# The steps of the late modulation sums, bound to their place in POOL's order

## The chip, the cores and the metric

The kernel runs on one core of a Trainium2 chip. The core has a matrix engine (PE, whose weight loads are shown apart as PEld), a vector engine (DVE), a scalar engine (ACT), a general engine (POOL) and a sync engine (SP) that here does nothing but issue transfers. Each engine takes its instructions strictly in the order in which they stand in its program; engines wait for each other, and for transfers, by semaphores. The metric is the time of one execution on the device in microseconds (us). Before the change the median of three runs is 1459.89 us (1458.16 to 1461.62).

## The reference

One layer of a diffusion backbone: two token mixers (differential attention and a multi-scale pooling) joined by gates, then an MLP with a squared ReLU. 256 latent tokens and 256 context tokens, width 2048, MLP width 8192, all in float32. Six vectors, computed from the conditioning vector `c`, shift, scale and gate the stream:

```python
mod = (jax.nn.silu(c) @ w_mod[l] + b_mod[l])[:, None, :]
sa, ca, ga, sm, cm, gm = jnp.split(mod, 6, axis=-1)
...
h = modulate(x, norm_attn_w[l], sa, ca)          # rmsnorm * (1 + ca) + sa
p = h @ w_in[l]
...
x = x + ga * mix
x = x + gm * sq_relu_mlp(modulate(x, norm_mlp_w[l], sm, cm), w_ff1[l], w_ff2[l])
```

`sa` and `ca` are needed at the very start. The other four, `ga`, `cm`, `sm` and `gm`, are needed late: `ga` when the mixed tokens have been projected, `cm` and `sm` for the second norm, `gm` in the last lines of the MLP. Each is a product of one row of 2048 with a 2048 x 2048 matrix; this document is about how these four are summed.

## The kernel before

**Products.** Every float32 weight tile is split in two parts: `whi` (rounded, by ACT, L245) and `wlo` (the rest, by DVE, L246). Three matmuls stand for one float32 product (high by high, low by high, high by low). PE reads the weights in chunks of 128 x 1024; `wchunk` loads, splits and hands out the next chunk, with two chunks of lookahead, six `raw` buffers for arriving weights and three buffers each for `whi` and `wlo`. All chunks stand in one list, `stream`, in the order of their use.

**Stages.** In order of time: the first products, which make the modulated input (to some 130 us); the products for v, q and k with the attention heads between them (to some 330 us); pooling; the gates, whose products are named `pg` and `pyy` (some 385 to 660 us); the output projection `wo` (to some 740 us); then the MLP, which goes through eight blocks. In a block, `ff1(b)` makes 1024 hidden columns in four parts: PE multiplies (L1035, L1038), ACT takes the ReLU (L1045), POOL squares it (`rsq`, L1046), ACT and DVE split the square (L272, L273) into the operand `act` for `ff2(b)`, which comes after (L454, L455, L460).

**The late sums.** `late_gen` works on `ga`, `cm`, `sm` and `gm` between the chunks of the main stream, half a vector (1024 columns) at a time. For each of 16 weight tiles, DVE adds `weights * silu(c)` to a 128 x 1024 tile (`late_part`, L628 and L630). That leaves 128 partial rows, which have to be added up across partitions. `late_fold` does that by transfers that add to their destination: rows 64 to 127 are added to rows 0 to 63, then 32 to 16, and so on down to one row (seven steps, L635); this row is added to a row in DRAM that holds the bias (L638), and the row is read back into all 128 partitions (L641). For `cm`, `late_norm` stands between these, with two transfers and two small POOL operations (L646 to L649). The tiles are `ga_bc` (both halves of `ga`), `sb` (`cm` and `sm`) and `gm_bc`. Each of the eight halves so needs nine transfers or more, every one of which has to land before the next can be issued. All are issued by POOL: a transfer that has to wait for the one before it makes all of POOL wait, and whatever stands behind it in POOL's program.

**What sets the order.** Steps of the fold are put off with `later(n, fn)`: `fn` runs after `n` more weight chunks have been handed out, and writes its instructions into the program at that place. A list scheduler then orders each engine's program by its own estimate of when each instruction is ready. An instruction wrapped in `pin` (`keep_in_program_order`) keeps its place with respect to the rest of the program instead. Before the change the `late_fold` transfers are not pinned. Most other work on POOL that the document speaks of is not pinned either: the rotary additions `qraw` (L485) and the squares `rsq`.

Of the kernel before, what the change touches and what calls it, by code (L numbers as in the profile page):

```python
# [14 lines left out]
ALU = mybir.AluOpType  # L15
AX = mybir.AxisListType

P = 128
# [30 lines left out]
def layer(ctx: ExitStack, tc, a, out):  # L49
    nc = tc.nc  # L50
# [4 lines left out]
    pin = tc.keep_in_program_order  # L55
# [41 lines left out]
    def later(n, fn):  # L97

        waiting.append([n, fn])
# [426 lines left out]
    cols = {}  # L526
# [70 lines left out]
    def late_gen():  # L597
        for name in ("ga", "cm", "sm", "gm"):
            if name == "ga":
                dst = ga_bc  # L600
            elif name == "gm":
                mods["gm"] = None
                yield
                mods["gm"] = s8("gm_bc", [P, D])
                dst = mods["gm"]
            else:
                if "sb" not in mods:
                    mods["sb"] = s16("sb", [P, 2, D])
                dst = mods["sb"][:, 0 if name == "cm" else 1, :]
            for half in range(2):  # L610
                yield
                o = dst[:, half * 1024:half * 1024 + 1024]
                norm_w = pr("nmw")[:, 8 * half:8 * half + 8] if name == "cm" else None
                for k in range(KT):
                    raw = raw_chunk(a["w_" + name][half, k])
                    later(2 if credit_rate[0] < 1 else 1, partial(late_part, o, raw, k))
                    if k == 8:
                        row = rows.tile([1, 1024], F32, tag="row", name="row")
                        nc.gpsimd.dma_start(row, a["b_" + name][half])
                    if k == KT - 1:  # L620
                        wait = 40 - 26 * half if name == "ga" else 2 if credit_rate[0] < 1 else 1
                        later(wait, partial(late_fold, o, row, norm_w, P // 2, 2 if name == "sm" else 3))
                    yield
# [8 lines left out]
    def late_fold(o, row, norm_w, n, step):  # L632

        if n > 0:
            nc.gpsimd.dma_start(o[0:n, :], o[n:2 * n, :], accum_op=ALU.add)  # L635
            later(step, partial(late_fold, o, row, norm_w, n // 2, step))
            return
        nc.gpsimd.dma_start(row, o[0:1, :], accum_op=ALU.add)  # L638
        if norm_w is not None:
            later(1, partial(late_norm, row, norm_w))  # L640
        later(2 if norm_w is None else 3, lambda: nc.gpsimd.dma_start(o, row.broadcast_to([P, 1024])))  # L641

    def late_norm(row, norm_w):

        cols = pool.tile([P, 8], F32, tag="nmc", name="nmc")
        nc.gpsimd.dma_start(cols, row.rearrange("o (p c) -> (o p) c", c=8))  # L646
        gp.tensor_scalar(cols, cols, 1.0, None, ALU.add)
        gp.tensor_mul(cols, cols, norm_w)
        nc.gpsimd.dma_start(row.rearrange("o (p c) -> (o p) c", c=8), cols)  # L649
# [536 lines left out]
```

## Time and profile before

| | |
|---|---|
| median of three runs | 1459.89 us |
| the profiled execution | 1465.34 us, with a span of 1463.6 us |
| granted clock of PE, mean over the span | 0.996 |
| busy share of DVE, ACT, POOL | 67%, 46%, 12% |
| bytes moved by transfers | 355.23 MB, 243 GB/s in the mean |

The page of a profile sums one execution; the views behind it list instructions by time, by line or by tile. In a list of instructions in order of time, the columns are the start (us from the span's start), the duration, the engine, the line and operation, output and input; in square brackets stands how long the engine sat idle before it, and what ended the wait. In a list of waits the columns are the total in us, the number of waits and the longest. Where a stretch of time is tabulated, each engine's busy time is followed by its count of instructions, and the last three columns are PE's granted clock (1.00 is full speed), the busy share of the 16 DMA engines and GB/s. POOL's transfers are shown with the time it takes to issue them, not to carry them out.

### The profile page before, as it was taken

How to read it: one execution, taken by the hardware profiler on the slowest of the kernel's cores; microseconds unless marked ns; L12 is line 12 of the kernel's file. 1: busy time of each engine (PE TensorE's matmuls, PEld its weight loads, DVE VectorE, ACT ScalarE, POOL GpSimd, SP SyncE). 2: the span in 40 equal slices, each digit the busy share in tenths (PEclk: the TensorE clock that was granted, in tenths of full speed). 3: DMA queues.
4: the chain of work that ended last, by engine and by line, in shares of the span. 5: the costliest groups of instructions: out<-in, count | busy, mean ns of one | idle time of the engine just before them, and what ended most of it. 6: DMA issues, size and time to landing. Idle time of an engine off the chain costs nothing.

```text
span 1463.6 us, 19756 instructions
## 1 busy us (share of the span) xinstructions
PE 1435.7 (98%) x7448; PEld 1181.9 (81%) x7448; DVE 983.3 (67%) x1218; ACT 670.4 (46%) x901; POOL 173.1 (12%) x192
## 2 busy tenths in 40 slices
PE   6999989999999999999999999999999999999998
PEld 4667877778888888888878888888888788888887
DVE  4567785668788778787767656656666465555675
ACT  4235335556654444444545545445354353544432
POOL 1001111102310121110101100110000100000260
PEclk9999999999999999999999999999999999999999
DMA  9996693335589999999646677777777665565563
GB/s 374 408 408 248 212 324 112 101 116 163 174 297 332 339 329 340 333 348 332 226 153 225 231 235 236 245 237 247 243 233 240 199 198 193 188 194 193 185 195 124
DMA packets 100976, 355.23 MB, mean 243 GB/s; under 512 B 12864, under 2 KB 13520, under 8 KB 100880
## 3 DMA queue, kind: packets, MB, share of 16 engines
q1 hardware_dynamic: 96624, 345.19, 68.5%
q0 software_dynamic: 4256, 8.77, 2.6%
q8 instruction: 58, 0.95, 0.3%
q14 instruction: 38, 0.31, 0.1%
HBM read 347.61 MB, written 2.17 MB: 239 GB/s over the span
## 4 chain that ended last, share of the span: by engine, by line
PE 84%; DMA 10%; issue 2%; DVE 1%; ACT 1%; POOL 1%; SPq 0%; DVEq 0%; POOLq 0%; ACTq 0%
PE f L1035 13%; PE f L455 8%; PE f L454 8%; PE f L460 8%; PE f L1038 7%; DMA raw<-in_w_m_dram 6%; PE pg L455 4%; PE pg L454 4%; PE pg L460 4%; DMA gm_bc<-gm_bc 2%; PE pyy L455 2%; PE v L455 2%; PE pyy L460 2%; PE pyy L454 2%; PE v L454 2%
## 5 line engine op out<-in xcount | busy, mean ns | idle before, releaser
L246 DVE TENSOR_TENSOR wlo<-raw,whi 128x1024 fp32r<-128x1024 f32 (+1 forms) x430 | 533.2, 1243 | 339.5 <-ACT whi L245 309.4
L245 ACT CAST whi<-raw 128x1024 fp32r<-128x1024 f32 (+1 forms) x430 | 449.9, 1047 | 558.4 <-PE f L455 184.7
L1035 PE MATMUL f<-h,whi 128*128 128x512 f32 x896 | 225.9, 395 | 3.1 <-ACT whi L245 3.1
L455 PE MATMUL f<-whi,act 128*128 128x512 f32 x512 | 199.5, 390 | 0.0
L454 PE MATMUL f<-whi,act 128*128 128x512 f32 x512 | 199.3, 389 | 0.0
L1035 PEld LDWEIGHTS f<-h,whi 128*128 128x128 f32 x896 | 162.6, 190 | 32.6 <-ACT whi L245 3.3
L460 PE MATMUL f<-wlo,act 128*128 128x512 f32 x512 | 136.9, 389 | 0.0
L1038 PEld LDWEIGHTS f<-h,wlo 128*128 128x128 f32 x896 | 122.6, 191 | 8.8
L1038 PE MATMUL f<-h,wlo 128*128 128x256 f32 x896 | 125.1, 283 | 0.0
L460 PEld LDWEIGHTS f<-wlo,act 128*128 128x128 f32 x512 | 96.1, 188 | 19.9
L455 PEld LDWEIGHTS f<-whi,act 128*128 128x128 f32 x512 | 96.2, 188 | 19.8
L454 PEld LDWEIGHTS f<-whi,act 128*128 128x128 f32 x512 | 96.1, 188 | 19.7
L454 PE MATMUL pg<-whi,hL 128*128 128x512 f32 x256 | 100.8, 394 | 0.0
L455 PE MATMUL pg<-whi,hL 128*128 128x512 f32 x256 | 99.8, 390 | 0.0
L1046 POOL TENSOR_TENSOR rsq<-relu 128x512 f32<-128x512 f32 x28 | 29.2, 1042 | 432.3 <-ACT relu L1045 422.1
L630 DVE SCALAR_TENSOR_TENSOR sb<-raw,sil,sb 128x1024 f32<-128x1024 f32 x60 | 76.8, 1280 | 0.0
L460 PE MATMUL pg<-wlo,hL 128*128 128x512 f32 x256 | 68.5, 389 | 0.0
L455 PEld LDWEIGHTS pg<-whi,hL 128*128 128x128 f32 x256 | 48.1, 188 | 10.1 <-issue 0.2
L454 PEld LDWEIGHTS pg<-whi,hL 128*128 128x128 f32 x256 | 48.1, 188 | 10.1 <-issue 0.2
L460 PEld LDWEIGHTS pg<-wlo,hL 128*128 128x128 f32 x256 | 48.1, 188 | 10.0
L1060 DVE TENSOR_TENSOR acc<-f,acc 128x512 f32<-128x512 f32 x48 | 30.9, 686 | 20.5 <-PE f L460 20.5
L635 POOL DMA_DIRECT2D sb<-sb x28 | 22.2, 791 | 186.7 <-DMA sb<-sb 121.2
(283 smaller groups left out, 2182.8 us busy)
## 6 DMA issues: line engine op xcount, KB each, us to landing
raw<-in_w_ff_dram SPq DMA_DIRECT2D x240, 512.0 KB, 4.2
raw<-in_w_m_dram SPq DMA_DIRECT2D x64, 512.0 KB, 10.2
raw<-in_w_ga_dram SPq DMA_DIRECT2D x32, 512.0 KB, 4.4
raw<-in_w_gb_in_dram SPq DMA_DIRECT2D x32, 512.0 KB, 5.1
raw<-in_w_cm_dram SPq DMA_DIRECT2D x32, 512.0 KB, 5.5
raw<-in_w_ga_in_dram SPq DMA_DIRECT2D x32, 512.0 KB, 5.5
raw<-in_w_sm_dram SPq DMA_DIRECT2D x32, 512.0 KB, 5.5
raw<-in_w_o_dram SPq DMA_DIRECT2D x32, 512.0 KB, 5.5
```

Source lines behind the costliest of these rows:

```text
L245: act.copy(hi, raw)
L246: vec.tensor_sub(lo, raw, hi.bitcast(F32))
L454: pe.matmul(banks[t], tok(h, k, 0, tt), wt, start=k == 0, stop=False)
L455: pe.matmul(banks[t], tok(h, k, 1, tt), wt, start=False, stop=False)
L460: pe.matmul(banks[t], tok(h, k, 0, tt), wt, start=False, stop=k == 2 * nk - 1)
L630: pin(vec.scalar_tensor_tensor(o, raw, sil[:, 0, k:k + 1], o, ALU.mult, ALU.add))
L635: nc.gpsimd.dma_start(o[0:n, :], o[n:2 * n, :], accum_op=ALU.add)
L1035: pe.matmul(ps, hi[:, kk * P:kk * P + P], both(h2, k), start=k == 0, stop=False)
L1038: pe.matmul(ps[:, T:2 * T], lo[:, kk * P:kk * P + P], act_slice(h2, k, 0), start=False, stop=k == KT - 1)
L1046: gp.tensor_mul(sq, r, r)
L1060: vec.tensor_add(acc[:, t, gs], bs[t], acc[:, t, gs])
```

## The change

All transfers of `late_fold` and the first of `late_norm` are wrapped in `pin`, so that they keep the place at which the program writes them. What is computed, the number of instructions and the operations are the same.

```diff
     def late_fold(o, row, norm_w, n, step):
         if n > 0:
-            nc.gpsimd.dma_start(o[0:n, :], o[n:2 * n, :], accum_op=ALU.add)
+            pin(nc.gpsimd.dma_start(o[0:n, :], o[n:2 * n, :], accum_op=ALU.add))
             later(step, partial(late_fold, o, row, norm_w, n // 2, step))
             return
-        nc.gpsimd.dma_start(row, o[0:1, :], accum_op=ALU.add)
+        pin(nc.gpsimd.dma_start(row, o[0:1, :], accum_op=ALU.add))
         if norm_w is not None:
             later(1, partial(late_norm, row, norm_w))
-        later(2 if norm_w is None else 3, lambda: nc.gpsimd.dma_start(o, row.broadcast_to([P, 1024])))
+        later(2 if norm_w is None else 3, lambda: pin(nc.gpsimd.dma_start(o, row.broadcast_to([P, 1024]))))

     def late_norm(row, norm_w):
         cols = pool.tile([P, 8], F32, tag="nmc", name="nmc")
-        nc.gpsimd.dma_start(cols, row.rearrange("o (p c) -> (o p) c", c=8))
+        pin(nc.gpsimd.dma_start(cols, row.rearrange("o (p c) -> (o p) c", c=8)))
```

The programs of PE, DVE, ACT and SP keep their order; only POOL's differs, in four places. The first two belong together. Before, the nine transfers of `ga`'s first half stand between the rotary additions of the second group of query heads; in POOL's program of before, that place reads (a number behind a name tells tiles of one name apart):

```order
L485 TENSOR_TENSOR qraw_1321<-qraw_1321,qsq_1323 128x512
L635 DMA ga_bc_1341<-ga_bc_1341 64x1024
L635 DMA ga_bc_1341<-ga_bc_1341 32x1024
L635 DMA ga_bc_1341<-ga_bc_1341 16x1024
L635 DMA ga_bc_1341<-ga_bc_1341 8x1024
L485 TENSOR_TENSOR qraw_1836<-qraw_1836,qsq_1838 128x512
L635 DMA ga_bc_1341<-ga_bc_1341 4x1024
L485 TENSOR_TENSOR qraw_1856<-qraw_1856,qsq_1858 128x512
L635 DMA ga_bc_1341<-ga_bc_1341 2x1024
```

In the changed program the additions follow each other, and the transfers of both halves of `ga` stand in the gates, alternating, behind the last POOL operation of the attention (`osq`); this is the head of that place in POOL's new program, where the first row of 64x1024 belongs to the first half and the second one to the second half:

```order
L728 TENSOR_SCALAR osq_3670<-osq_3670 128x512
L635 DMA ga_bc_1341<-ga_bc_1341 64x1024
L635 DMA ga_bc_1341<-ga_bc_1341 32x1024
L635 DMA ga_bc_1341<-ga_bc_1341 16x1024
L635 DMA ga_bc_1341<-ga_bc_1341 8x1024
L635 DMA ga_bc_1341<-ga_bc_1341 64x1024
L635 DMA ga_bc_1341<-ga_bc_1341 4x1024
L635 DMA ga_bc_1341<-ga_bc_1341 32x1024
L635 DMA ga_bc_1341<-ga_bc_1341 2x1024
L635 DMA ga_bc_1341<-ga_bc_1341 16x1024
```

So nine transfers have moved from the attention to the gates, from before two rotary additions to a place where POOL computes nothing. The end of the second half (its last addition, its row, its broadcast) has moved behind the first transfers of `sb`.

The third and fourth places are the two folds of `gm_bc` in the MLP. Before, the second one stands in one piece ahead of four squares of an MLP block; in POOL's program of before:

```order
L635 DMA gm_bc_6622<-gm_bc_6622 4x1024
L635 DMA gm_bc_6622<-gm_bc_6622 2x1024
L635 DMA gm_bc_6622<-gm_bc_6622 1x16x64
L638 DMA row_9067<-gm_bc_6622 16x1x64
L641 DMA gm_bc_6622<-row_9067 128x1024
L1046 TENSOR_TENSOR rsq2_9978<-relu_9979 128x512
L1046 TENSOR_TENSOR rsq2_10082<-relu_10083 128x512
L1046 TENSOR_TENSOR rsq2_10187<-relu_10188 128x512
```

In the changed program the same transfers stand between the squares:

```order
L635 DMA gm_bc_6622<-gm_bc_6622 8x1024
L1046 TENSOR_TENSOR rsq2_9978<-relu_9979 128x512
L635 DMA gm_bc_6622<-gm_bc_6622 4x1024
L1046 TENSOR_TENSOR rsq2_10082<-relu_10083 128x512
L635 DMA gm_bc_6622<-gm_bc_6622 2x1024
L635 DMA gm_bc_6622<-gm_bc_6622 1x16x64
L1046 TENSOR_TENSOR rsq2_10187<-relu_10188 128x512
L638 DMA row_9067<-gm_bc_6622 16x1x64
L1046 TENSOR_TENSOR rsq2_10291<-relu_10292 128x512
L641 DMA gm_bc_6622<-row_9067 128x1024
```

Five of the nine steps have moved behind one or more of the block's squares. The first fold of `gm_bc` moves in the same way, by four steps.

## The prediction

> **What bounds the kernel now.** I read the page first, then PE's list of waits, then the lists in order of time around each wait. The page says that PE is the engine that counts; its waits say where time can still be won.
>
> ```profile
> span 1463.6 us, 19756 instructions
> PE 1435.7 (98%) x7448; PEld 1181.9 (81%) x7448; DVE 983.3 (67%) x1218; ACT 670.4 (46%) x901; POOL 173.1 (12%) x192
> ...
> PE qkT L492 <- POOL qraw L485: 4.0, 1, 4.0
> PE f L1035 <- ACT whi L245: 3.1, 1, 3.1
> ```
>
> PE is idle for 1463.6 - 1435.7 = 27.9 us. Most of that lies at the start and the end, where the change does nothing. Behind the first 130 us the list has two waits of weight, 4.0 and 3.1 us, each of them a single event. The first one names POOL. The second names ACT, and has to be followed back to whom ACT waited for.
>
> **The first wait.** Here are DVE's rotary product that feeds the fifth addition, the rows of POOL around that addition, and PE's.
>
> ```profile
> 207.28 0.69 DVE L484 TENSOR_TENSOR qraw<-qraw,tabs 128x512 f32<-128x512 f32 x1
> ...
> 198.19 0.90 POOL L635 DMA_DIRECT2D ga_bc<-ga_bc  x1 [39.77 <-DMA raw<-in_w_ga_dram]
> ...
> 216.69 0.81 POOL L635 DMA_DIRECT2D ga_bc<-ga_bc  x1 [3.75 <-DMA ga_bc<-ga_bc]
> 217.24 1.55 POOL L485 TENSOR_TENSOR qraw<-qraw,qsq 128x512 f32<-128x512 f32 x1
> ...
> 213.72 1.13 PE L693 MATMUL sc<-kT,qT 64*128 64x512 f32 x4
> 218.85 0.79 PE L492 MATMUL qkT<-prm,qraw 128*128 128x128 f32 x4 [4.00 <-POOL qraw L485]
> 219.29 0.77 PE L454 MATMUL k<-whi,hL 128*128 128x512 f32 x1
> 219.86 0.63 PE L455 MATMUL k<-whi,hL 128*128 128x512 f32 x1
> 220.29 0.63 PE L454 MATMUL k<-whi,hL 128*128 128x512 f32 x1
> ...
> 222.77 0.39 PE L454 MATMUL k<-whi,hL 128*128 128x512 f32 x1
> 223.00 0.39 PE L455 MATMUL k<-whi,hL 128*128 128x512 f32 x1
> ```
>
> The addition's data were there at 207.28 + 0.69 = 207.97 us. It ran at 217.24, since four transfers of the fold stood ahead of it, from 198.19 to 216.69, each waiting until the last had landed. PE wanted its transposes at 213.72 + 1.13 = 214.85 and got them at 218.85. Then it ran slow for a while: matmuls started 0.43 us apart (219.86, 220.29), and 0.23 us apart later (222.77, 223.00). From 218.85 to 222.77 it did four transposes and eight matmuls in 3.92 us; at full speed the eight take 8 x 0.23 = 1.84, and with the 0.55 us or so that I estimate for the transposes the same work is 2.4. So the wait cost 4.0 + 1.5 = 5.5 us. With the transfers gone the addition can run from 208.0 to 209.5, over 5 us before PE asks. What is late next? The transposes stand behind `sc`, which is PE's own work, so nothing is left to wait for there: **-5.5 us**.
>
> **The second wait.** ACT waits in the MLP, for POOL:
>
> ```profile
> 1071.31 1.04 POOL L1046 TENSOR_TENSOR rsq<-relu 128x512 f32<-128x512 f32 x1 [53.65 <-ACT relu L1045]
> 1082.48 1.04 POOL L1046 TENSOR_TENSOR rsq<-relu 128x512 f32<-128x512 f32 x1 [10.13 <-ACT relu L1045]
> ...
> 1129.74 0.85 POOL L635 DMA_DIRECT2D gm_bc<-gm_bc  x1 [23.87 <-DVE gm_bc L630]
> ...
> 1167.95 0.58 POOL L641 DMA_DIRECT2D gm_bc<-row  x1 [1.59 <-DMA row<-gm_bc]
> 1168.54 1.06 POOL L1046 TENSOR_TENSOR rsq<-relu 128x512 f32<-128x512 f32 x1
> ...
> 1252.66 1.04 POOL L1046 TENSOR_TENSOR rsq<-relu 128x512 f32<-128x512 f32 x1 [53.65 <-ACT relu L1045]
> ...
> 1340.87 1.04 POOL L1046 TENSOR_TENSOR rsq<-relu 128x512 f32<-128x512 f32 x1 [53.65 <-ACT relu L1045]
> ...
> 1169.63 0.62 ACT L272 CAST act<-rsq 128x512 fp32r<-128x512 f32 x1 [9.31 <-POOL rsq L1046]
> ...
> 1171.25 3.54 PE L1035 MATMUL f<-h,whi 128*128 128x512 f32 x8 [3.09 <-ACT whi L245]
> ...
> 1175.71 2.00 PE L1035 MATMUL f<-h,whi 128*128 128x512 f32 x8
> ```
>
> The first square of an MLP block comes every 88.21 us when nothing is in the way (1340.87 - 1252.66). After the one at 1071.31 the next was due at 1159.5. It came at 1168.54, 9.0 us late, because the whole fold, from 1129.74 to 1167.95, stood ahead. ACT's split of that square was 9.31 us late, ACT's cast of the next weights stood behind the split, and PE waited 3.09 us and then took 3.54 us for eight matmuls that take 2.00. What it cost in all is read from the blocks: 1252.66 - 1071.31 = 181.35, against 2 x 88.21 = 176.42: 4.9 us. With the new order the first square stands behind the step of eight rows. The fold starts at 1129.74, and four steps of some 5 us each (the median of a landing is 5.1, quoted below) end by 1150, before 1159.5. Each later square has at most two steps ahead of it, and the squares come 11.17 us apart (1082.48 - 1071.31): **-4.9 us**. What hides the waits that the change adds here (a square behind a step) is this gap: it is gone if one step takes over 5 us longer than it does now. The fold ends some 30 us later than now, near 1200.
>
> The first fold of `gm_bc` has the same shape, yet PE's list shows no wait for it:
>
> ```profile
> 985.03 1.06 POOL L1046 TENSOR_TENSOR rsq<-relu 128x512 f32<-128x512 f32 x1
> ...
> 986.12 0.62 ACT L272 CAST act<-rsq 128x512 fp32r<-128x512 f32 x1 [2.23 <-POOL rsq L1046]
> ```
>
> There ACT was held up by 2.23 us only, and PE's weights were split ahead by more than that. Nothing is to be had: 0.
>
> **What the moved transfers cost where they go.** Nine transfers land in the gates, beside those of the second half.
>
> ```profile
> q0 software_dynamic: 4256, 8.77, 2.6%
> ...
> 416.00:420.00 4.00, 4.00 (x19) 3.34 (x18) 4.00 (x5) 1.80 (x2) 0.17 (x1) 1.00 0.80 260
> 420.00:424.00 4.00, 4.00 (x19) 3.30 (x19) 3.67 (x4) 1.05 (x1) 0.60 (x1) 1.00 0.83 272
> 424.00:428.00 4.00, 4.00 (x20) 3.30 (x19) 3.07 (x5) 1.97 (x2) 0.78 (x1) 1.00 0.90 352
> ...
> 425.70 1.05 ACT L245 CAST whi<-raw 128x1024 fp32r<-128x1024 f32 x1 [3.50 <-PE pg L460]
> ...
> 428.22 0.39 PE L454 MATMUL pg<-whi,hL 128*128 128x512 f32 x1
> ...
> 540.85 1.05 ACT L245 CAST whi<-raw 128x1024 fp32r<-128x1024 f32 x1 [1.66 <-PE pg L455]
> ...
> 547.00 0.39 PE L454 MATMUL pyy<-whi,yb 128*128 128x512 f32 x1
> ...
> L898 DVE TENSOR_TENSOR xtmp<-wo,ga_bc x6: 683/688/693, 676.4 to 723.0; 128x512 f32<-128x512 f32 x6
> ```
>
> POOL's queue (q0) takes 2.6% of the span of all 16 DMA engines, 38 us, for eight halves: at most 4.8 us a half. I counted ACT's casts against PE's chunks through the gates: the cast that ends at 426.75 is for the chunk that PE starts at 428.22. That margin of 1.47 us is the smallest of the stage; the cast that ends at 541.90 is for the chunk of 547.00, 5.1 us ahead, and most are so from there on. In the changed order the large steps of the second half (64 and 32 rows) fall there, at about 416 to 428, since the halves now take turns. They are the larger part of the 4.8 us; from 416 to 428 the DMA engines have 0.8 + 0.7 + 0.4 = 1.9 us to spare. My estimate is 2.5 us of extra transfer work, against 1.9 + 1.47 = 3.4 to hide it: nothing is left over, and I take 0. The other bound: all 4.8 us arrive late, PE waits 4.8 - 1.5 = 3.3 us, and 1.7 us of slow clock follow, **+5.0 us**. A gain there I exclude, since PE does not idle in the gates now. `ga` is late next, but has time: its first reader (L898) starts at 676, and the second half's broadcast, now behind two steps of `sb`, should be out by 490. `sb` itself loses a microsecond or two to the transfers put between its own, and each of its halves starts with DVE's next sum, not with the fold before.
>
> **The sum** is -5.5 - 4.9 = -10.4 us: 1465.34 - 10.4 = 1454.9 in a profiled execution. The profiled one is 5.45 us above the median of the runs shown. I take the change off that median: 1459.89 - 10.4 = **1449.5 us**.
>
> **A rule weighed.** The rows show PE slowed after both waits, 0.43 for 0.23 us after 4.00 us of idleness, 3.54 for 2.00 after 3.09. The Trainium skill ("TensorE: Matmul & The Clock Gate", Part 1) has the clock fall to half after an idle window of about 3.4 us, and says elsewhere that gaps over some 3 us are to be avoided. By the longer figure the second wait would have cost no clock, and the sum would be 5.5 + 3.1 = 8.6 us. The trace has a slow start after 3.09 us, and I go by it.
>
> **Rivals.**
> (a) *The loads in the gates fall behind by some of that bound.* For it: the margin of 1.47 us, and DMA shares of 0.8 to 0.9. Against it: PE idles nowhere in the gates now, though two folds of `sb` run there. Half of the 5.0 gives 1452.0; all of it 1454.5.
> (b) *The waits are smaller without the profiler.* The runs are 5.45 us shorter than the profiled execution. If all of that is shorter transfers ahead of the two POOL operations, only 10.4 - 5.45 = 5.0 us can be won: 1454.9. Against it: it would have to spare all the other work.
> (c) *The change finds nothing to remove.* A step of the fold takes some 5 us to land:
>
> ```profile
> DMA to landing us min/median/max: 2.1/5.1/9.8
> ```
>
> The second fold has eight landings ahead of the square, which is 9.0 us late, of which some 4 us are hidden; 0.6 us less a landing would undo the wait: 1459.9. The Trainium skill ("DMA: Bandwidth & Descriptors", Anatomy of one DMA) has about 2.0 us and the bytes at 436 GB/s for such a transfer; by that rule both waits would be gone in the runs, and the change worth nothing. The trace's median disagrees with it here.
> (d) *Slower: two folds under way slow every weight load.* The median from issue to landing is 4.4 us for `ga`'s weights, most of which load while no fold is under way, and 5.5 for the gates':
>
> ```profile
> raw<-in_w_ga_dram SPq DMA_DIRECT2D x32, 512.0 KB, 4.4
> ...
> raw<-in_w_ga_in_dram SPq DMA_DIRECT2D x32, 512.0 KB, 5.5
> ```
>
> Should a second chain add another 1.1 us, the six `raw` buffers, each in use for some 10 us (an estimate: two loads in each 2.7 us chunk at most, less in part), would turn over 11% slower for the 94 us from 396 to 490: 10.3 us, less 1.5 of margin, and several slow starts of 1.5 us, say four: +15 us, 1464.5. It decides from a loss of 10.4 us, some 0.8 us a load over the whole stretch. Against it: beside the folds of `sb` the casts keep 5.1 us ahead after 540.
>
> **How the numbers follow.** Forecast (1449.5, itself 1447.5 to 1451.5): 0.64. (a): 0.16. (b): 0.09. (c): 0.06. (d): 0.05. A range from 1447 to 1456 holds the forecast, (a) and (b), nearly 9 in 10; it could only be narrower by dropping (a)'s bound. What a measurement of this kernel can tell from no change is about 0.2%, 2.9 us. Faster by more: 0.64 + 0.16 + 0.08 of (b) = 0.88; (c) and the rest of (b) within it, 0.07; slower, 0.05.
>
> **What would show it.** Right: PE's list of waits has lost both rows; a `qraw` addition runs near 208 us, right after DVE's product; the squares come 88.2 us apart throughout; `ga_bc`'s transfers start near 397 and alternate; granted clock 1.00 where it was below. Wrong: a wait of PE for `whi` or of ACT for `raw` between 410 and 500 (a, d); a square that waits behind a landing in the MLP; a trace with both waits gone and runs that do not follow it (b, c).

## The result, and the profile after

| | before | after |
|---|---|---|
| median of the timed runs | 1461.09 us (5 runs, 1458.16 to 1462.74) | 1454.14 us (5 runs, 1453.27 to 1454.52) |
| the profiled execution | 1465.34 us | 1453.27 us |
| ratio of the runs, 95% interval | | 0.9954 [0.9939, 0.9968] |

The change makes the kernel faster by 6.95 us in the median; by the ratio of the runs it is 0.46%, so the effect is small, but its interval lies clear of 1. The forecast was 10.4 us and 1449.5 us. The result is 4.64 us above that: 3.45 us because the gain is smaller, and 1.2 because the median of five runs of before is that much above the median of three from which the forecast set out. The two profiled executions differ by 12.1 us. So there are two different gains to explain, and the gap between them is what the experiments are about.

Here are the first lines of the page of the changed kernel and PE's whole list of waits:

```profile
span 1451.5 us, 19755 instructions
...
PE 1431.9 (99%) x7448; PEld 1179.1 (81%) x7448; DVE 982.5 (68%) x1218; ACT 670.6 (46%) x901; POOL 172.0 (12%) x192
...
PE ssq L68 <- DVE sq L68: 10.8, 3, 6.7
PE mod L68 <- DMA raw<-in_w_m_dram: 2.1, 5, 0.6
PE pin L278 <- DVE wlo L246: 0.7, 1, 0.7
PE modT L68 <- DVE blocks L68: 0.6, 1, 0.6
PE qkT L492 <- ACT e L698: 0.5, 1, 0.5
```

Both rows are gone, `qkT <- POOL qraw` (4.0) and `f <- ACT whi` (3.1), and no other has come in their place. PE is busy for 3.8 us less (1435.7 to 1431.9) at the same count of matmuls; 3.5 of that are the slow clock behind the two waits, by what each cost beyond its idle time (5.68 - 4.00 and 4.91 - 3.09, worked out below). Now POOL's list of the changed kernel in order of time, around the first place:

```profile
135.23 2.20 POOL L485 TENSOR_TENSOR qraw<-qraw,qsq 128x512 f32<-128x512 f32 x1 [46.18 <-DVE rq_t L288]
...
207.53 1.58 POOL L485 TENSOR_TENSOR qraw<-qraw,qsq 128x512 f32<-128x512 f32 x1 [50.06 <-PE k L460]
211.77 2.15 POOL L485 TENSOR_TENSOR qraw<-qraw,qsq 128x512 f32<-128x512 f32 x1 [2.67 <-DVE qraw L484]
255.67 1.29 POOL L485 TENSOR_TENSOR qraw<-qraw,qsq 128x512 f32<-128x512 f32 x1 [41.75 <-DVE rq_t L288]
```

The fifth addition runs at 207.53 us, where it ran at 217.24. The first row and the last are the first additions of the first and of the third group of heads. Both wait for data only, so the stretch between them tells what the wait cost. It is 255.67 - 135.23 = 120.44 us now. Before, the same two additions stood here:

```profile
136.19 2.20 POOL L485 TENSOR_TENSOR qraw<-qraw,qsq 128x512 f32<-128x512 f32 x1 [46.24 <-DVE rq_t L288]
...
262.31 1.29 POOL L485 TENSOR_TENSOR qraw<-qraw,qsq 128x512 f32<-128x512 f32 x1 [29.91 <-DVE rq_t L288]
```

That is 126.12 us: the first wait cost 5.68 us in that execution. The squares and the second fold of `gm_bc`, again in POOL's list of the changed kernel:

```profile
1064.13 1.04 POOL L1046 TENSOR_TENSOR rsq<-relu 128x512 f32<-128x512 f32 x1 [53.65 <-ACT relu L1045]
...
1122.56 0.86 POOL L635 DMA_DIRECT2D gm_bc<-gm_bc  x1 [23.87 <-DVE gm_bc L630]
1129.73 0.77 POOL L635 DMA_DIRECT2D gm_bc<-gm_bc  x1 [6.31 <-DMA gm_bc<-gm_bc]
1135.01 0.75 POOL L635 DMA_DIRECT2D gm_bc<-gm_bc  x1 [4.51 <-DMA gm_bc<-gm_bc]
1139.93 0.80 POOL L635 DMA_DIRECT2D gm_bc<-gm_bc  x1 [4.16 <-DMA gm_bc<-gm_bc]
1152.35 1.03 POOL L1046 TENSOR_TENSOR rsq<-relu 128x512 f32<-128x512 f32 x1 [11.62 <-ACT relu L1045]
1153.34 0.81 POOL L635 DMA_DIRECT2D gm_bc<-gm_bc  x1
1163.52 1.04 POOL L1046 TENSOR_TENSOR rsq<-relu 128x512 f32<-128x512 f32 x1 [9.37 <-ACT relu L1045]
...
1186.87 0.60 POOL L641 DMA_DIRECT2D gm_bc<-row  x1
...
1240.57 1.03 POOL L1046 TENSOR_TENSOR rsq<-relu 128x512 f32<-128x512 f32 x1 [53.10 <-ACT relu L1045]
```

The square at 1152.35 follows the one at 1064.13 by 88.22 us and waits for its ReLU, not for a transfer. Two blocks take 1240.57 - 1064.13 = 176.44 us, where they took 181.35: the second wait cost 4.9 us in that execution. The fold ends at 1186.87, some 19 us later than before (1167.95), and nobody waits for it.

So 12.1 us of difference between the two profiled executions are 5.68 and 4.91 for the two waits, 0.96 of an earlier start (the additions at 136.19 and 135.23) and 0.5 in between (262.31 to 1071.31 is 809.00 us, 255.67 to 1064.13 is 808.46).

In the gates, the first of `ga`'s moved transfers stand so in POOL's list:

```profile
389.98 0.89 POOL L635 DMA_DIRECT2D ga_bc<-ga_bc  x1
395.23 0.80 POOL L635 DMA_DIRECT2D ga_bc<-ga_bc  x1 [4.36 <-DMA ga_bc<-ga_bc]
```

The table by stretches of time has the load there:

```profile
408.00:416.00 8.00, 8.00 (x37) 6.64 (x36) 6.97 (x8) 4.32 (x5) 2.39 (x3) 1.00 0.97 275
416.00:424.00 8.00, 8.00 (x37) 6.64 (x36) 7.03 (x7) 2.23 (x3) 1.56 (x2) 1.00 1.00 365
424.00:432.00 8.00, 8.00 (x37) 6.61 (x36) 6.54 (x7) 3.04 (x3) 2.31 (x4) 1.00 0.99 333
```

The DMA share (the last column but one) is 0.97 to 1.00, against 0.80 to 0.90 from 416 to 428 before. PE is busy for the whole of each stretch at a clock of 1.00. In this execution the room that the prediction counted on has been used up, and no more than that. ACT's casts and PE's chunks show how close it came:

```profile
439.25 1.05 ACT L245 CAST whi<-raw 128x1024 fp32r<-128x1024 f32 x1 [3.49 <-DMA raw<-in_w_a_dram]
...
440.62 0.39 PE L454 MATMUL pyy<-whi,oT 128*128 128x512 f32 x1
```

Counted chunk by chunk as before, the cast that ends at 440.30 is for the chunk of 440.62. Between these two executions the smallest margin has gone from 1.47 to 0.32 us.

### The profile page after: what moved, and what is told of

Read it like the earlier page. It is cut to its first block, busy times and chain, and to the rows that moved or that the text cites. A ratio compares the mean times of both kernels' runs of the same rounds, so it can differ in the third digit from the quotient of the medians.

```text
span 1451.5 us, 19755 instructions
## 1 busy us (share of the span) xinstructions
PE 1431.9 (99%) x7448; PEld 1179.1 (81%) x7448; DVE 982.5 (68%) x1218; ACT 670.6 (46%) x901; POOL 172.0 (12%) x192
## 3 DMA queue, kind: packets, MB, share of 16 engines
q0 software_dynamic: 4256, 8.77, 2.7%
## 4 chain that ended last, share of the span: by engine, by line
PE 91%; DMA 7%; DVE 1%; ACT 0%; issue 0%; POOL 0%; SPq 0%; DVEq 0%
PE f L1035 14%; PE f L455 8%; PE f L454 8%; PE f L460 8%; PE f L1038 7%; DMA raw<-in_w_m_dram 6%; PE pg L454 4%; PE pg L455 4%; PE pg L460 4%; PE pyy L454 2%; PE pyy L455 2%; PE pyy L460 2%; PE v L455 2%; PE v L454 2%; PE v L460 2%; PE wo L454 2%
```

## The experiments

**Theory A**: the two waits go with the times that the chained transfers take to land, and these differ from one execution to the next; the profiled execution of before had long ones. **Theory B**: the two waits cost about 10 us in every execution, and the changed kernel gives part of the gain back in the gates.

The first four kernels ran together, with 29 timed runs of the kernel before beside them: 1461.64 us in the median, 1458.73 to 1465.98.

### The kernel before, once more

No edit.

> The kernel of before, unchanged, for a second profile. Theory A (the two waits depend on how long eight or nine landings take in a row, and so differ from one execution to the next; the execution profiled first had large ones): PE's waits on qraw and on whi differ from 4.0 and 3.1 us by 1 us or more each way, and the execution's time moves with their sum and the slow starts behind them. Theory B (the waits are the same in every execution, and the runs of the changed kernel give some of the gain back in the gates): 4.0 and 3.1 us again within 0.5, time beyond the median of before by no more than 2 us.

Measured: 1461.40 us in the median of 12 (1457.95 to 1465.16), ratio 0.9998 [0.9986, 1.0009]. The profiled execution took 1461.54 us, 3.8 us less than the first one. PE's wait for `qraw` is 3.82 us in it, where A expected a difference of 1 us or more in both waits; its wait for `whi` is 0.87. The end of the second fold in POOL's list, and PE's list behind it:

```profile
1165.71 0.58 POOL L641 DMA_DIRECT2D gm_bc<-row  x1 [2.29 <-DMA row<-gm_bc]
1166.30 1.06 POOL L1046 TENSOR_TENSOR rsq<-relu 128x512 f32<-128x512 f32 x1
...
1169.01 2.11 PE L1035 MATMUL f<-h,whi 128*128 128x512 f32 x8 [0.87 <-ACT whi L245]
```

The fold started at 1129.73, as in the first execution (1129.74), and was through at 1165.71, where it had been 1167.95. The square was 2.2 us less late, PE waited 2.2 us less, and the eight matmuls took 2.11 us in place of 3.54. The same program, the same order: only the landings were quicker. This is what A says, for the second wait.

The first wait idles PE for nearly as long as in the first execution, and yet costs more: the two additions that enclose it are 262.11 - 135.17 = 126.94 us apart, 6.50 over the changed kernel's 120.44. PE's list shows matmuls that are slow for longer:

```profile
217.65 1.12 PE L492 MATMUL qkT<-prm,qraw 128*128 128x128 f32 x4 [3.82 <-POOL qraw L485]
...
222.40 0.63 PE L455 MATMUL k<-whi,hL 128*128 128x512 f32 x1
...
223.24 0.39 PE L455 MATMUL k<-whi,hL 128*128 128x512 f32 x1
```

The granted clock is 0.50 from about 216.4 to 223.2 us here, 6.8 us, of which PE works for 5.55; in the first execution it is 0.50 from 219.2 to 222.7, 3.4 us. So the cost of a wait differs by its slow start too.

### Only `ga`'s folds pinned, and only `gm`'s

```diff
-    later(wait, partial(late_fold, o, row, norm_w, P // 2, 2 if name == "sm" else 3))
+    later(wait, partial(late_fold, o, row, norm_w, P // 2, 2 if name == "sm" else 3, pin if name in ('ga',) else lambda x: x))
...
-            nc.gpsimd.dma_start(o[0:n, :], o[n:2 * n, :], accum_op=ALU.add)
+            hold(nc.gpsimd.dma_start(o[0:n, :], o[n:2 * n, :], accum_op=ALU.add))
```

`hold` is that last argument; the other kernel has `('gm',)`.

> Only the two folds of ga are bound to their place; gm as before. Theory A: the profile shows no wait on qraw, the wait on whi near 1160 us stays; time 3 to 4 us below before (about half of the 7.0 us that the whole change gave). Theory B: the time lost in the gates is all in this half, so 5.5 less 3.4, about 2 us below before.

> Only the two folds of gm are bound to their place; ga as before. Theory A: the wait on qraw stays, the squares come 88.2 us apart throughout; time 3 to 4 us below before. Theory B: the full 4.9 us below before, since nothing is added in the gates.

| | median (12 runs each) | ratio to before | PE waits in its profile |
|---|---|---|---|
| only `ga` | 1457.49 us (1454.41 to 1460.61) | 0.9968 [0.9956, 0.9980] | `whi` 3.4 |
| only `gm` | 1459.44 us (1456.30 to 1461.45) | 0.9983 [0.9973, 0.9994] | `qraw` 3.8 |

Each half of the change takes away its own wait and leaves the other. In the median `ga`'s half is worth 4.15 us and `gm`'s 2.2, which is less than 5.5 and 4.9. A expected 3 to 4 us of each, so 4.15 lies a little above and 2.2 below; B's 2 and 4.9 lie outside both intervals. Their twelve runs each are spread over 6.2 and 5.2 us, the six of the next kernel, which has neither wait, over 1.6. With one wait left, the spread is still there; so both waits differ from run to run, not the second alone. In the one with `ga` alone the second wait happened to be the longest that was traced. PE's list of it:

```profile
1166.52 3.68 PE L1035 MATMUL f<-h,whi 128*128 128x512 f32 x8 [3.44 <-ACT whi L245]
```

### The changed kernel, with `ga`'s first half folded during the attention

```diff
-    wait = 40 - 26 * half if name == "ga" else 2 if credit_rate[0] < 1 else 1
+    wait = (14 if half else 14) if name == "ga" else 2 if credit_rate[0] < 1 else 1
```

The first half's steps so stand from 261.69 us on, behind the additions, and the gates have only the second half to carry.

> The changed kernel with the fold of ga's first half put at 14 chunks behind its sum in place of 40, so that its steps lie between 260 and 390 us and the gates have only the fold of the second half, as before. Theory A: the time of the changed kernel within 1 us (7 us below before); the smallest margin of a weight cast ahead of PE in the gates goes back from 0.3 us to about 1.5. Theory B: 10 us below before, since what the gates took is given back.

Measured: 1453.48 us in the median of 6 (1452.86 to 1454.50), ratio 0.9946 [0.9934, 0.9959]; the profiled execution took 1453.52. The gates' DMA share is 0.78 from 408 to 416 here, 0.97 in the changed kernel; the smallest margin of a cast ahead of PE is 2.05 us, where A expected some 1.5; and the time is within 0.7 us of the changed kernel's, which ran in other groups. If the gates had taken back 3.5 us, as B says, these would show as a gain here: 10 us below before is a ratio of 0.9932, just outside the interval. The trace of the changed kernel says so too: from 400 to 660 us PE is busy for all 260.00 us at a clock of 1.00. B falls. This order leaves the gates more room, but no run tells it from the changed kernel in time.

The last four kernels ran in a second group, with 20 timed runs of before beside them: 1460.99 us in the median, 1458.81 to 1464.46.

### One landing fewer ahead of the squares, in the order of before

```diff
-    later(wait, partial(late_fold, o, row, norm_w, P // 2, 2 if name == "sm" else 3))
+    later(wait, partial(late_fold, o, row, norm_w, P // 4 if name == "gm" else P // 2, 2 if name == "sm" else 3))
```

> The kernel before, with gm's folds begun at 32 rows in place of 64 (rows 64 to 127 of gm's sums are left out): one landing fewer ahead of the squares, every order as before. Theory A (the second wait is the chain of landings, of which 5.9 us of lateness are hidden): the first square of the second fold comes about 4 to 5 us less late, so 2 to 5 us late, no wait of PE for whi, squares 176.4 us apart over two blocks; time like the one with only gm's folds pinned, 2 to 3 us under before (ratio 0.998 to 0.9985). Rival (in the timed runs that wait costs nothing, and what pinning gm's folds won came from elsewhere): ratio 1.000.

Measured: 1459.16 us in the median of 11 (1457.29 to 1462.00), ratio 0.9990 [0.9979, 1.0000]; the profiled execution took 1459.02. The squares in POOL's list:

```profile
1069.94 1.04 POOL L1046 TENSOR_TENSOR rsq<-relu 128x512 f32<-128x512 f32 x1 [53.65 <-ACT relu L1045]
...
1160.33 0.58 POOL L641 DMA_DIRECT2D gm_bc<-row  x1 [3.27 <-DMA row<-gm_bc]
1160.92 1.06 POOL L1046 TENSOR_TENSOR rsq<-relu 128x512 f32<-128x512 f32 x1
...
1246.37 1.04 POOL L1046 TENSOR_TENSOR rsq<-relu 128x512 f32<-128x512 f32 x1 [53.65 <-ACT relu L1045]
```

The first square was due at 1069.94 + 88.21 = 1158.15 and came 2.77 us late; PE's list has no wait for `whi`, and two blocks take 176.43 us. One landing decides over the whole wait, as A expected, and 2.77 us of lateness cost nothing. In the runs it is worth 1.8 us, a little under the 2 to 3 that A expected; the interval ends at 1.000, so this result alone does not exclude the rival. The one with only `gm` pinned does (0.9983, up to 0.9994).

### The large steps of `ga` doubled in the gates

```diff
-            pin(nc.gpsimd.dma_start(o[0:n, :], o[n:2 * n, :], accum_op=ALU.add))
+            for _ in range(2 if step == 3 and late_name[0] != "gm" and norm_w is None and n > 16 else 1):
+                pin(nc.gpsimd.dma_start(o[0:n, :], o[n:2 * n, :], accum_op=ALU.add))
```

`late_name` holds the name at which `late_gen` is; with it, the condition selects `ga`'s steps of 64 and 32 rows.

> The changed kernel, with ga's steps of 64 and 32 rows issued twice (their rows are added twice, so ga is not the reference's): some 4 to 5 us more of transfers in the gates, and two landings more in each of ga's chains. If the gates have next to nothing to spare (the least margin of the casts ahead of PE is 0.32 us in the changed kernel): PE waits for whi there by 1 to 4 us, and with slow starts the time is 2 to 6 us above the changed kernel. Rival (the margin shrinks only as far as it is free, loads catch up): no wait in the gates, time within 1 us of the changed kernel.

Measured: 1455.39 us in the median of 10 (1453.92 to 1459.33), 1.65 us above the changed kernel in the same group. That lies between the two expectations (2 to 6 us, and within 1), a little nearer to the first. The profiled execution took 1456.62 us. PE's waits for weights in the gates, from PE's list of it:

```profile
432.94 0.50 PE L454 MATMUL pg<-whi,hL 128*128 128x512 f32 x1 [0.34 <-ACT whi L245]
...
439.12 0.50 PE L454 MATMUL pyy<-whi,oT 128*128 128x512 f32 x1 [0.44 <-ACT whi L245]
...
468.89 0.50 PE L454 MATMUL pg<-whi,hL 128*128 128x512 f32 x1 [1.22 <-ACT whi L245]
```

They are 2.0 us together, and no matmul behind them is slow (0.50 and then 0.40). So the gates are near their limit in the changed kernel: more transfers there are paid for, though less than one for one. POOL's queue moved 9.56 MB here and 8.77 in the changed kernel, where that took 2.7% of the span; by that the 0.79 MB more are some 3.5 us of transfers, an estimate, and the 1.65 us are about half of it.

### The changed kernel, once more

No edit.

> The changed kernel unaltered, beside the others of this call. Theory A (its spread is small because both waits are gone): 1453.3 to 1454.6 in the timed runs, and a profiled execution within 1 us of 1453.3. Rival (the spread comes from elsewhere): a spread of 5 us or more, as before has.

Measured: 1453.74 us in the median of 5 (1453.20 to 1455.38), ratio 0.9955 [0.9942, 0.9967]; the profiled execution took 1454.35. One run lies 0.8 us above the range that A gave, one 0.1 below it, and the profiled one 0.05 above its own range. The spread of 2.2 us over five runs, against 5.7 over the 20 of before beside them, speaks for A.

### The kernel before, a third time

No edit.

> The kernel before unaltered, one more profiled execution. Theory A (the second wait differs from one execution to the next, the first hardly): PE's wait for qraw 3.5 to 4.2 us; its wait for whi anywhere from 0 to 3.5 us, equal to the lateness of the first square less 5.9 us. Rival (the waits are the same each time): 4.0 and 3.1 us.

Measured: 1459.96 us. From PE's list of waits:

```profile
PE qkT L492 <- POOL qraw L485: 2.4, 1, 2.4
PE f L1035 <- ACT whi L245: 1.9, 1, 1.9
```

And POOL's list in order of time, up to the addition for which PE waits:

```profile
197.00 0.90 POOL L635 DMA_DIRECT2D ga_bc<-ga_bc  x1 [39.13 <-DMA raw<-in_w_k_dram]
204.56 0.80 POOL L635 DMA_DIRECT2D ga_bc<-ga_bc  x1 [6.67 <-DMA ga_bc<-ga_bc]
210.50 0.76 POOL L635 DMA_DIRECT2D ga_bc<-ga_bc  x1 [5.13 <-DMA ga_bc<-ga_bc]
214.55 0.81 POOL L635 DMA_DIRECT2D ga_bc<-ga_bc  x1 [3.29 <-DVE wlo L246]
215.10 1.55 POOL L485 TENSOR_TENSOR qraw<-qraw,qsq 128x512 f32<-128x512 f32 x1
```

The first wait is 2.4 us here, not 3.5 to 4.2: my expectation that it hardly differs was wrong. The four steps took 17.6 us from the first issue to the last (197.00 to 214.55), where they had taken 18.5 (198.19 to 216.69). The row of 214.55 names DVE's `wlo`, which ended at about that time; but the trace has the third step landed at 214.27, and each issue of the chain follows the landing before it by some 0.3 us, so it is the landing that counts. The second wait agrees: the square was 1164.70 - (1068.66 + 88.21) = 7.83 us late, less 5.9 is 1.9.

### All executions side by side

For each profiled execution, the cost of the first wait is its stretch between the two additions less 120.44 us, and that of the second is its two blocks less 176.43:

| execution | time | first wait: PE idle, cost | square late by | second wait: PE idle, cost | time less both costs |
|---|---|---|---|---|---|
| before, the first | 1465.34 | 4.00, 5.68 | 9.02 | 3.09, 4.92 | 1454.7 |
| before, once more | 1461.54 | 3.82, 6.50 | 6.79 | 0.87, 1.13 | 1453.9 |
| before, a third time | 1459.96 | 2.42, 4.13 | 7.83 | 1.90, 2.16 | 1453.7 |
| only `ga` pinned | 1460.61 | none, 0.0 | 9.37 | 3.44, 5.26 | 1455.4 |
| only `gm` pinned | 1458.97 | 3.82, 5.53 | 0 | none, 0.0 | 1453.4 |
| one landing fewer | 1459.02 | 3.82, 5.49 | 2.77 | none, 0.0 | 1453.5 |
| `ga`'s first half early | 1453.52 | none, 0.0 | 0 | none, 0.0 | 1453.5 |
| after, the first | 1453.27 | none, 0.0 | 0 | none, 0.0 | 1453.3 |
| after, once more | 1454.35 | none, 0.0 | 0 | none, 0.0 | 1454.4 |

The kernel with `ga`'s large steps doubled is not in the table: it has neither wait, and its 1456.62 us hold the 2.0 us of waits in the gates instead. The last column is the point: less the cost of its two waits, every execution takes 1453.3 to 1455.4 us, which is what the changed kernel takes. Times that lie 12 us apart come together within 2.1. The fourth column less the wait is 5.9 wherever there is a second wait (9.02 - 3.09, 6.79 - 0.87, 7.83 - 1.90, 9.37 - 3.44 are 5.93, 5.92, 5.93, 5.93).

## Why the prediction came out as it did

**The first wait, -5.5.** Right in its cause, and in its size for that execution (5.68). In the five traces that hold it, it cost 4.13 to 6.50 us, 5.5 in the mean, so that the first execution was no exception here. In the runs `ga`'s half is worth 4.15 us when it is done alone, and 5.96 when `gm`'s is done already (1459.44 less 1453.48, the median of the kernel with `ga`'s first half early, which stands for the changed one in that group).

**The second wait, -4.9.** Right in its cause, and in its size for that execution (4.92). In the four traces that hold it, it cost 1.13 to 5.26 us, 3.4 in the mean: this is the term that the one execution shows too large. In the runs it is worth 2.2 us alone, and 4.0 when `ga`'s half is done already (1457.49 less 1453.48). The intervals of these ratios are 1.5 to 1.8 us wide to each side, so whether the two parts add up stays open; the whole is 6.95 to 8.2 us in three comparisons.

**The sum, and the step that failed.** Each term was read from one execution whose waits were large, and then came the sentence "I take the change off that median". That is the step: the median run of before does not contain 10.4 us of waits. It contains some 7 to 8: that is what the three comparisons of medians give in which both waits go; the larger part of what is missing belongs to the second wait, by the two means above and by both ways of taking the halves. Of the 29 runs of before in the first group, only one, at 1465.98, is above the first profiled execution; that execution held an unusually costly pair of waits. The prediction noted that it was 5.45 us above the median, and did not ask what the 5.45 were. Had the sum been made against the execution alone, 1465.34 - 10.4, it would have read 1454.9, a figure the prediction wrote down and passed over, 0.8 us above the result. The measured 1454.14 us lies above the 1447.5 to 1451.5 that the forecast itself was given, in the part of the range that was kept for (a) and (b). Neither of these named the cause, so it is in part luck that the range holds the result.

**Some 4 us hidden.** Mis-sized: 5.9 us are hidden, in four executions of four. It did not enter the sum, but it enters (c): not 0.6 but 0.4 us less a landing ((9.02 - 5.93) / 8) would undo the second wait. And it decides how steep the second wait is: between 5.9 and 9.4 us of lateness the cost goes from 0 to 5.3.

**The gates, 0.** Right, and near the edge. Neither profiled execution of the changed kernel waits there, and folding the first half earlier gains nothing that can be measured. The prediction had margin and room together as just enough; what was left of 1.47 us was 0.32. That too is one draw: counted in the same way, the smallest margin is 0.73 to 1.52 us in the five executions whose gates are those of before, 0.32 and 1.12 in the two of the changed kernel, and 0.05 with only `ga` pinned. It is smaller after the change, but by how much differs. The place was somewhat off: the first transfers were put near 397 us and start at 389.98, and by the order of POOL's program the second half's steps of 64 and 32 rows were issued between 405 and 412, not between 416 and 428. Doubling the large steps on top of the change costs 1.65 us, still below the bound of 5.0.

**The first fold of `gm`, 0.** Right; the stretch between the two places is 0.5 us shorter at most.

**The cover of the new waits.** Right: four steps end before the square is due, the steps behind a square fit into the gap, and the squares stay 11.17 us apart (1152.35, 1163.52). The fold ends some 19 us later, not 30, and without a reader in wait.

**The rule weighed.** By the Trainium skill ("TensorE: Matmul & The Clock Gate", Part 1) an idle window of about 3.4 us sets the clock back. The eight matmuls behind the second wait took 3.54 us after 3.09 of idleness and 3.68 after 3.44, but 2.11 after 0.87 and after 1.90, where 2.00 is full speed. So the slow start was rightly counted in the first execution, and absent in others: one wait 1.2 us longer costs 2.8 more (2.16 to 4.92). The 8.6 us that the prediction worked out for no slow start there are nearer to the runs than 10.4, but not for that reason: the clock did fall after 3.09 us.

**Rivals.** (a) did not happen: no waits in the gates. (b) gave 1454.9 and had the right consequence, waits that are smaller in most runs, with the wrong cause: it laid this on the profiler, yet the three profiled executions of before hold 10.6, 7.6 and 6.3 us of waits. (c) fell: the first wait is there in all three and in the two others that keep it, the second in all four that keep it. The Trainium skill ("DMA: Bandwidth & Descriptors", Anatomy of one DMA) would have a step of 256 KB land after about 2.6 us, an estimate by its 2.0 us and the bytes at 436 GB/s; the third execution of before has 7.6 between the issues of the first and the second step (197.00 and 204.56), while the DMA engines were fully busy (a share of 1.02), so the rule was too short for that step. (d) fell: the gates' weights land after 5.7 us in the median, where it needed 6.6.

Three things stay open. Why the landings differ between executions of one program was not tried. What decides whether PE's clock falls behind a wait, and for how long, is not shown. And what each wait was in a timed run is not known one by one; it is inferred from spreads and from executions with traces.

## What to carry to other kernels

A wait read from one trace is one draw: before its size is taken off a median, compare the profiled execution's own time with the timed runs, and where they differ, put the difference down to the variable waits first, or make the sum against the profiled execution alone. An engine that has to wait for chained transfers should do so behind its urgent work, since in that order a late landing costs nothing, while the other order costs time and makes runs differ. When transfers are moved to a fuller stage, count the margin there after the move as well, in more than one trace: zero cost with 0.3 us left in one and 1.1 in another is a limit, not a reserve.

## What the hardware showed that was not expected

One program's chained transfers land at different times from one execution to the next: eight landings ahead of the square took from 35.98 us (1129.73 to 1165.71) to 38.56 (1124.66 to 1163.22) in four executions.

PE's clock does not depend on the length of a wait alone. After 1.90 us of idleness in the MLP it stayed fast; after 2.42 us in the attention, in the same execution (before, a third time), it did not, and not at once. PE's list:

```profile
216.71 0.66 PE L492 MATMUL qkT<-prm,qraw 128*128 128x128 f32 x4 [2.42 <-POOL qraw L485]
217.12 0.48 PE L454 MATMUL k<-whi,hL 128*128 128x512 f32 x1
217.44 0.39 PE L455 MATMUL k<-whi,hL 128*128 128x512 f32 x1
217.67 0.40 PE L454 MATMUL k<-whi,hL 128*128 128x512 f32 x1
217.91 0.54 PE L455 MATMUL k<-whi,hL 128*128 128x512 f32 x1
218.24 0.63 PE L454 MATMUL k<-whi,hC 128*128 128x512 f32 x1
...
221.23 0.48 PE L455 MATMUL k<-whi,hL 128*128 128x512 f32 x1
221.55 0.39 PE L454 MATMUL k<-whi,hC 128*128 128x512 f32 x1
```

Three matmuls ran at full speed behind the wait, and from about 218 to 221.4 us they were slow, some 3.4 us long. After 3.82 us of idleness the clock was low for 3.4 us in two executions (only `gm` pinned, and one landing fewer), and for 6.8, twice that, in a third (before, once more). The Trainium skill ("TensorE: Matmul & The Clock Gate", Part 1) describes windows of 3413 ns that run freely, whatever the program does. Slow stretches of that length or twice that length, one of which begins over 1 us after the wait, fit such windows; that 2.42 us of idleness within one are enough, it does not say.
